# Two partial sums per PSUM bank in the wide projections of a hybrid layer, and one modulation vector accumulated on GpSimd

## The chip, the cores and the metric

The kernel runs on one core of one Trainium2 chip. The metric is the device time of one execution in microseconds, as the median of several runs. TensorE multiplies, VectorE and ScalarE work elementwise, GpSimd does small side jobs, and SyncE's queue issues nearly all loads.

## The reference

One layer of a diffusion backbone over 256 latent and 256 context tokens with 2048 channels, in float32:

```python
mod = silu_c @ w_mod[l] + b_mod[l]
sh1, sc1, g1, sh2, sc2, g2 = (t[:, None, :] for t in jnp.split(mod, 6, axis=-1))
...
hx = modulate(rms_norm(x, norm1_g[l]), sh1, sc1)
out_x, _, _ = token_mixer(hx, *mix_args, s_f, s_b, True)
x = x + g1 * out_x
x = x + g2 * conv_ffn(modulate(rms_norm(x, norm2_g[l]), sh2, sc2),
                      w_up[l], ffn_dw[l], ffn_db[l], w_down[l], True)
...
return rms_norm(x, final_g)
```

The mixer multiplies the tokens with w_in (13312 columns), runs a gated linear recurrence over eight heads in both directions (branch A) and a short convolution (branch B), projects both with w_pa and w_pb, merges them by sigmoid gates and projects with w_o. The FFN multiplies with w_up (2 x 5632 columns), convolves one half over the token grid, multiplies the halves and projects with w_down.

## The kernel before

Every weight is used once. wload asks for a raw tile of 1 MB (four buffers); wsplit cuts each half of it into an exact high part (w_hi, ScalarE, line 90) and the low rest (w_lo, VectorE, line 91), five buffers each. The tokens are kept in two such parts too: hx[:, k, 0, :] and hx[:, k, 1, :] lie side by side, 256 tokens each. A product needs three matmuls, which mm3 issues: low weights with high tokens, high weights with high tokens, high weights with low tokens. In proj the weights are stationary (128 x 128) and 256 tokens move; 16 tiles k of 128 rows sum into one PSUM tile acc of [128, 2, 256], one bank, that holds two blocks n of 128 output channels. A bank is 512 floats wide. Six banks (pool psA) rotate for all products, two (psH) serve small ones.

The program runs in stages: norm 1 and modulated gates of the first heads (zacc); four rounds g of the recurrence for two heads each (hgrn), in which gate products (acx, lines 365 to 378), q (proj, line 586) and values (vacc, moving operand 512 columns) fill TensorE between the recurrence's own small products (kdt, ps, po, pn); branch B and the branch A gate (four steps j of four proj calls); the merge (eight steps j with two branches each: one proj of 16 tiles over w_in, one of 8 over w_pa or w_pb); w_o with the residual and norm 2 (tiles to, 512 columns moving); the FFN's up projection (22 steps j, two proj calls each); w_down. A scheduler of the framework sets each engine's order within and across stages, by its own estimate of times; it is in order per engine at run time.

The second half's modulation vectors (segments 4, 3, 2, 5 of w_mod) are summed row by row: mod_steps loads a raw tile of 128 rows, VectorE adds raw times a scalar to macc (line 617), and pump advances it by one tile at places between the products. Segment 5, the gate g2, falls into the steps j = 2 to 17 of the FFN's up projection; then macc is split, spread over the partitions on TensorE and copied (lines 631 to 637).

Of the kernel before, what the change touches and what calls it, by code (L numbers as in the profile page):

```python
# [36 lines left out]
def hybrid_layer_kernel(ctx: ExitStack, tc: tile.TileContext, I, out, dbg=None):  # L37
# [9 lines left out]
    # Pools that live to the end.  # L47
# [5 lines left out]
    psA = ctx.enter_context(tc.tile_pool(name="psA", bufs=6, space=PSUM))  # L53
    psH = ctx.enter_context(tc.tile_pool(name="psH", bufs=2, space=PSUM))

# [4 lines left out]
    # ---------------------------------------------------------------- weights  # L60
# [89 lines left out]
    # =============================================================== startup  # L150
# [6 lines left out]
    # parameters as rows of 128, transposed to one value per partition  # L157
# [48 lines left out]
    # norm 1 of the latent and the context tokens, then channels on partitions  # L206
# [28 lines left out]
    # modulation of norm 1 in blocks of 256 channels, and with each block the products that it feeds:  # L235
    # backward gates of heads 0 to 3, forward gates of heads 0 to 2
# [8 lines left out]
    def mod_block(b):  # L245
        """shift and scale of block b as partial sums in 4 groups of 32 partitions"""
# [14 lines left out]
    def h_block(b, pm):  # L261
        """modulated tokens of the channels of block b"""
# [20 lines left out]
    def block_products(b, halves):  # L283
        """the products of block b, one output tile of 2 times 256 tokens at a time"""
# [40 lines left out]
    # lower bounds of the forget gates: softmax over the two rows  # L325
# [54 lines left out]
    def proj_xc1(w, c0):  # L380
        """One tile of 128 output channels for the latent and the context tokens."""
# [16 lines left out]
    def gate_evac(acc, dst):  # L398
        """sigmoid of the forget gate of one head and direction"""
        nc.scalar.activation(dst, acc[:], AF.Sigmoid)  # L400

    def q_evac(acc):
# [22 lines left out]
    def hgrn(g, ft, q):  # L425
        """Heads 2g and 2g+1. ft: sigmoids of the gates [direction, latent/context, head, token]."""
# [7 lines left out]
        # log f in two ranges of the logarithm, whose sum is exact where one is 0  # L434
# [12 lines left out]
        # final states of the context  # L447
# [29 lines left out]
        # scores [s, t] of both directions, by levels of the highest bit in which s and t differ;  # L477
        # up to the sixth level blocks of 64 by 64, two of them side by side in the array
# [25 lines left out]
        for lev in range(8):  # L504
# [28 lines left out]
            # halves join: exclusive sums take the whole of the other half, then the inclusive ones  # L533
# [31 lines left out]
    # gates of heads 2 and 3 wait in the part of v that is written last  # L565
    early = {}
    for g in range(4):
# [18 lines left out]
        q = q_evac(proj(w_in, [256 * g], hx, KD)[0])  # L586
# [22 lines left out]
    # modulations of the second half: sums over the rows within a partition, then over the partitions  # L609
    def mod_steps():  # L610
        for seg in (4, 3, 2, 5):
# [3 lines left out]
            for k in range(KD):  # L615
                raw = wload([(w_mod[k * P:k * P + P, seg * D:seg * D + D], (2048,))])
                nc.vector.scalar_tensor_tensor(out=acc[:], in0=raw[:], scalar=cst[:, k, 0:1], in1=acc[:], op0=ALU.mult, op1=ALU.add)  # L617
# [29 lines left out]
    for j in range(4):  # L647
        pc0, = proj(w_in, [6 * AW + 256 * j], hx, KD)
        u = tp.tile([P, 2, T], F32, name="u", tag="u")
        nc.scalar.copy(u[:], pc0[:])  # L650
        pump(1)
        pc1, = proj(w_in, [7 * AW + 256 * j], hx, KD)
        nc.vector.tensor_tensor(out=u[:], in0=u[:], in1=pc1[:], op=ALU.mult)
# [8 lines left out]
        nc.vector.tensor_tensor(out=cv[:], in0=cv[:], in1=pc2[:], op=ALU.mult)  # L662
        split((y_b[:, 2 * j:2 * j + 2, 0, :], y_b[:, 2 * j:2 * j + 2, 1, :]), cv[:])
        pump(1)
        pc3, = proj(w_in, [4 * AW + 256 * j], hx, KD)
        sg = tp.tile([P, 2, T], F32, name="sg", tag="sg")
        nc.scalar.activation(sg[:], pc3[:], AF.Sigmoid)
        nc.vector.tensor_tensor(out=sg[:], in0=sg[:], in1=pc3[:], op=ALU.mult)
# [6 lines left out]
    # merge of the branches  # L675
    w_pa = I["w_pa"][0]
    w_pb = I["w_pb"][0]
    for j in range(8):
        mb = []
        for i, (c0, w, y) in enumerate(((8 * AW, w_pa, y_a), (8 * AW + D, w_pb, y_b))):  # L680
            pg, = proj(w_in, [c0 + 256 * j], hx, KD)
            sg = tp.tile([P, 2, T], F32, name=f"sm{i}", tag=("u", "cv")[i])
            last_sigmoid = nc.scalar.activation(sg[:], pg[:], AF.Sigmoid)
            pump(2)
            pp, = proj(w, [256 * j], y, 8)
            nc.vector.tensor_tensor(out=sg[:], in0=sg[:], in1=pp[:], op=ALU.mult)
# [5 lines left out]
    tp_cm.__exit__(None, None, None)  # L692

    # ============================================================ w_o, the residual and norm 2
# [82 lines left out]
    def warm_sqrt(after):  # L777
        """the table of the square root, loaded while nothing waits for it"""
# [48 lines left out]
    # ============================================================ gated conv FFN  # L827
# [5 lines left out]
    for j in range(NF // 2):  # L833
# [4 lines left out]
        nc.scalar.copy(av[:], pa_[:])  # L838
# [93 lines left out]
```

## Time and profile before

| what | value |
|---|---|
| runs | 1776.76, 1777.16, 1778.48 us (median 1777.16) |
| span of the profiled execution | 1776.6 us |
| TensorE busy | 1746.4 us (98%), 13207 matmuls |
| VectorE busy | 1263.8 us (71%) |
| ScalarE busy | 857.3 us (48%) |
| GpSimd busy | 21.3 us (1%) |
| HBM | 381.20 MB read, 216 GB/s over the span |
| mean granted TensorE clock | 0.993 |

The profiled execution is known by its span alone, from its first to its last instruction; the median of the runs lies 0.6 us above it. A row of a group reads: line, engine, operation, output<-input, shapes, count, then busy time and mean length of one, then idle time of the engine ahead of it and what ended it. Matmul rows overlap each other, so a matmul's length is no pace. A row of a timeline begins with start and length in us.

### The profile page before, as it was taken

Reading aid. Unit: us, or ns where it says so; the run is one execution under the profiler, and the core shown is the slowest. Engines: PE = TensorE matmul, PEld = TensorE weight load, DVE = VectorE, ACT = ScalarE, POOL = GpSimd, SP = SyncE. Lnnn points to the kernel's source line nnn. Section 1 sums busy time; section 2 is a strip of 40 time slices with the busy share of each in tenths; the row PEclk is TensorE's granted clock in tenths of the full one; section 3 lists DMA queues with packets and bytes.
Section 4 is the critical chain, followed back from the end, with each engine's and each line's share of the span. In section 5 each row is a group of like instructions: output and inputs, shape, how many; then the busy total and the mean of one; then the engine's idle time right before and its main releaser. Section 6 shows DMA issues by size and latency. Waiting matters only on the chain.

```text
span 1776.6 us, 31077 instructions
## 1 busy us (share of the span) xinstructions
PE 1746.4 (98%) x13207; PEld 1641.1 (92%) x13207; DVE 1263.8 (71%) x1601; ACT 857.3 (48%) x1062; POOL 21.3 (1%) x26
## 2 busy tenths in 40 slices
PE   5999999999999999999999999999999999999998
PEld 3779889999999999999998899999999999888887
DVE  4337276677998768767865588778778877877774
ACT  4226255466555434434454454444444454665553
POOL 0000000000000000000000000000000000000000
PEclk9999999999999999999999999999999999999999
DMA  9996224223877879879976367767766755555552
GB/s 334 345 331 211 95 72 119 72 96 119 284 239 254 271 244 310 295 257 313 313 278 215 119 215 236 231 224 234 238 227 225 236 190 190 190 190 190 196 192 86
DMA packets 289008, 385.30 MB, mean 217 GB/s; under 512 B 7812, under 2 KB 241581, under 8 KB 280038
## 3 DMA queue, kind: packets, MB, share of 16 engines
q1 hardware_dynamic: 287872, 379.82, 64.3%
q10 hardware_dynamic: 694, 3.24, 0.5%
q8 instruction: 103, 1.69, 0.4%
q0 software_dynamic: 304, 0.26, 0.1%
q14 instruction: 35, 0.29, 0.0%
HBM read 381.20 MB, written 2.10 MB: 216 GB/s over the span
## 4 chain that ended last, share of the span: by engine, by line
PE 98%; DMA 0%; ACT 0%; DVE 0%; issue 0%; SPq 0%; ACTq 0%
PE acc L110 57%; PE to L110 19%; PE acx L110 6%; PE vacc L110 5%; PE zacc L110 5%; PE pm L110 2%; PE ps L110 2%; PE po L110 1%; PE pt L225 1%; DMA xt<-in_x_dram 0%; PE pc L110 0%; PE kdt L463 0%; PE ptx L798 0%; ACT hx L213 0%; PE pn L110 0%
## 5 line engine op out<-in xcount | busy, mean ns | idle before, releaser
L110 PE MATMUL acc<-hx,w_hi 128*128 128x256 f32 x5120 | 928.4, 284 | 0.0
L91 DVE TENSOR_TENSOR w_lo<-raw,w_hi 128x1024 fp32r<-128x1024 f32 (+1 forms) x521 | 633.4, 1219 | 269.7 <-ACT w_hi L90 266.2
L90 ACT ACTIVATE w_hi<-raw 128x1024 fp32r<-128x1024 f32 (+1 forms) x522 | 549.5, 1054 | 562.4 <-PE acc L110 360.4
L110 PEld LDWEIGHTS acc<-hx,w_hi 128*128 128x128 f32 x5120 | 802.9, 193 | 0.8
L110 PE MATMUL acc<-hx,w_lo 128*128 128x256 f32 x2560 | 727.9, 284 | 1.4 <-ACT hx L815 1.4
L110 PEld LDWEIGHTS acc<-hx,w_lo 128*128 128x128 f32 x2560 | 494.0, 193 | 1.9 <-issue 1.6
L110 PE MATMUL to<-w_hi,hx 128*128 128x512 f32 (+1 forms) x792 | 221.6, 366 | 0.0
L617 DVE SCALAR_TENSOR_TENSOR macc<-raw,cst,macc 128x2048 f32<-128x2048 f32 x64 | 150.3, 2348 | 30.6 <-DMA raw<-in_w_mod_dram 22.7
L110 PEld LDWEIGHTS to<-w_hi,hx 128*128 128x128 f32 x792 | 142.9, 188 | 24.4
L853 DVE SCALAR_TENSOR_TENSOR cvf<-av,pf,cvf 128x189 f32<-128x189 f32 (+2 forms) x352 | 132.6, 429 | 35.7 <-ACT cvf L841 35.7
L110 PE MATMUL to<-w_lo,hx 128*128 128x512 f32 (+1 forms) x396 | 145.1, 366 | 0.0
L106 ACT ACTIVATE hx<-y 128x512 fp32r<-128x512 f32 x88 | 55.5, 631 | 89.2 <-PE to L110 87.0
L110 PEld LDWEIGHTS to<-w_lo,hx 128*128 128x128 f32 x396 | 74.6, 188 | 12.0
L107 DVE TENSOR_TENSOR hx<-y,hx 128x512 fp32r<-128x512 f32 x88 | 60.7, 692 | 34.1 <-ACT hx L106 34.1
L110 PE MATMUL to<-w_hi,mg 128*128 128x512 f32 (+1 forms) x288 | 82.0, 368 | 0.0
L110 PE MATMUL acx<-hx,w_hi 128*128 128x256 f32 x288 | 61.1, 289 | 0.0
L110 PEld LDWEIGHTS to<-w_hi,mg 128*128 128x128 f32 x288 | 51.8, 188 | 8.7
L110 PE MATMUL acx<-hc,w_hi 128*128 128x256 f32 x288 | 58.6, 285 | 0.0
L110 PE MATMUL to<-w_lo,mg 128*128 128x512 f32 (+1 forms) x144 | 52.8, 366 | 0.0
L110 PE MATMUL zacc<-hx,w_hi 128*128 128x256 f32 x224 | 52.2, 289 | 0.0
L110 PE MATMUL acc<-y_b,w_hi 128*128 128x256 f32 x256 | 47.9, 289 | 0.0
L110 PE MATMUL zacc<-hc,w_hi 128*128 128x256 f32 x224 | 47.1, 287 | 0.0
(229 smaller groups left out, 1771.7 us busy)
## 6 DMA issues: line engine op xcount, KB each, us to landing
raw<-in_w_up_dram SPq DMA_DIRECT2D x88, 1024.0 KB, 5.2
raw<-in_w_in_dram SPq DMA_DIRECT2D x81, 1024.0 KB, 5.9
raw<-in_w_mod_dram SPq DMA_DIRECT2D x64, 1024.0 KB, 6.4
raw<-in_w_down_dram SPq DMA_DIRECT2D x44, 1024.0 KB, 5.0
raw<-in_w_mod_dram SPq DMA_DIRECT2D x64, 512.0 KB, 6.9
raw<-in_w_o_dram SPq DMA_DIRECT2D x16, 1024.0 KB, 5.4
raw<-in_w_in_dram SPq DMA_DIRECT2D x24, 512.0 KB, 4.3
raw<-in_w_pa_dram SPq DMA_DIRECT2D x8, 1024.0 KB, 5.8
```

The source lines that it names most:

```text
L90: nc.scalar.activation(hi[:, :n], half, AF.Copy)
L91: sub.tensor_tensor(out=lo[:, :n], in0=half, in1=hi[:, :n].bitcast(F32), op=ALU.subtract)
L106: nc.scalar.activation(dst[0], src, AF.Copy)
L107: nc.vector.tensor_tensor(out=dst[1], in0=src, in1=dst[0].bitcast(F32), op=ALU.subtract)
L110: return nc.tensor.matmul(o, lhsT, rhs, start=start, stop=stop, skip_group_check=True)
L225: nc.tensor.transpose(pt[:, k, :], xts[2 * i + t][k4 // 2][:, kk * P:kk * P + P], ident[:])
L617: nc.vector.scalar_tensor_tensor(out=acc[:], in0=raw[:], scalar=cst[:, k, 0:1], in1=acc[:], op0=ALU.mult, op1=ALU.add)
L853: nc.vector.scalar_tensor_tensor(out=c4[:, ro, co], in0=a4[:, ri, ci], scalar=pf[:, tap * NF + f:tap * NF + f + 1], in1=c4[:, ro, co], op0 ...
```

## The change

mm2 takes the place of mm3 in proj: one matmul of the high weights over both token parts (512 columns, a whole bank), and one of the low weights over the high tokens (256 columns), which adds to the second half of that bank. A product therefore leaves two sums side by side, and an accumulator of two blocks n takes two banks. joined brings the sums together: ScalarE copies the second, VectorE adds the first. The gate products and values keep mm3 and psA's six banks; q has a projection of its own, proj_q, with one bank per block; from the end of the recurrence on, the six banks are three double ones (psW), again six single ones for w_o (psB), three double ones for the FFN's up projection (psF) and six for w_down (psD). The convolution's first tap in branch B moves to ScalarE. For segment 5, GpSimd scales the raw tile in place and adds it to macc.

```diff
+    def mm2(o, wl, wh, s, start, stop):
+        mm(o, wh, s, start, False)
+        mm(o[:, T:2 * T], wl, s[:, 0, :], False, stop)
+
+    def joined(dst, acc):
+        nc.scalar.copy(dst, acc[:, :, 1, :])
+        nc.vector.tensor_tensor(out=dst, in0=acc[:, :, 0, :], in1=dst, op=ALU.add)
...
     def proj(w, cols, src, kt):
-            acc = psA.tile([P, 2, T], F32, name="acc", tag="acc")
+            acc = psW.tile([P, 2, 2, T], F32, name="acc", tag="acw")
...
                         for n in range(2):
-                            mm3(acc[:, n, :], lv[:, n * P:n * P + P], hv[:, n * P:n * P + P],
-                                src[:, kk, 1, :], src[:, kk, 0, :], kk == 0 and n == 0, kk == kt - 1)
+                            mm2(acc[:, n].rearrange("p a b -> p (a b)"), lv[:, n * P:n * P + P], hv[:, n * P:n * P + P],
+                                src[:, kk], kk == 0, kk == kt - 1)
+    def proj_q(c0):
+        accs = []
+        for n in range(2):
+            acc = psA.tile([P, 2, T], F32, name="acc", tag="acc")
+            accs.append(acc)
...
+    def q_evac(accs):
         q = gp.tile([P, 2, T], F32, name="q", tag="q", bufs=2)
-        nc.scalar.activation(q[:], acc[:], AF.Sigmoid)
-        nc.vector.tensor_tensor(out=q[:], in0=q[:], in1=acc[:], op=ALU.mult)
+        for n, acc in enumerate(accs):
+            nc.scalar.copy(q[:, n, :], acc[:, 1, :])
+            nc.vector.tensor_tensor(out=q[:, n, :], in0=acc[:, 0, :], in1=q[:, n, :], op=ALU.add)
+        sg = g2.tile([P, 2, T], F32, name="sq", tag="qq")
+        nc.scalar.activation(sg[:], q[:], AF.Sigmoid)
+        nc.vector.tensor_tensor(out=q[:], in0=q[:], in1=sg[:], op=ALU.mult)
...
+    psA_cm.__exit__(None, None, None)
+    psW_cm, psW = banks("psW", 3)
...
-                nc.vector.scalar_tensor_tensor(out=acc[:], in0=raw[:], scalar=cst[:, k, 0:1], in1=acc[:], op0=ALU.mult, op1=ALU.add)
+                if seg == 5:
+                    nc.gpsimd.tensor_scalar(out=raw[:], in0=raw[:], scalar1=cst[:, k, 0:1], scalar2=None, op0=ALU.mult)
+                    nc.gpsimd.tensor_tensor(out=acc[:], in0=raw[:], in1=acc[:], op=ALU.add)
+                else:
+                    nc.vector.scalar_tensor_tensor(out=acc[:], in0=raw[:], scalar=cst[:, k, 0:1], in1=acc[:], op0=ALU.mult, op1=ALU.add)
...
-            nc.vector.tensor_scalar(out=cv[:, n, :], in0=u[:, n, :], scalar1=w[1], scalar2=None, op0=ALU.mult)
+            nc.scalar.activation(cv[:, n, :], u[:, n, :], AF.Copy, scale=w[1])
...
-        nc.scalar.copy(av[:], pa_[:])
+        joined(av[:], pa_)
...
-        nc.vector.tensor_tensor(out=yj, in0=yj, in1=pb_[:], op=ALU.mult)
+        bv = tw.tile([P, 2, T], F32, name="bv", tag="bv")
+        joined(bv[:], pb_)
+        nc.vector.tensor_tensor(out=yj, in0=yj, in1=bv[:], op=ALU.mult)
```

Every other product of proj is joined in the same way (into u, z or sg) before its first use.

The order of VectorE in round g = 3 of the recurrence, from the last gate (ft, line 431, line 465 after) to the operand of the transposes kdt (line 457, line 491 after). Its middle, before:

```order
L563 TENSOR_TENSOR o_n<-po,r 128x512
L91 TENSOR_TENSOR w_lo<-raw,w_hi 128x1024
L405 TENSOR_TENSOR q<-q,acc 128x512
L91 TENSOR_TENSOR w_lo<-raw,w_hi 128x1024
L443 TENSOR_TENSOR X<-X,ft 128x1024
L444 TENSOR_TENSOR gc<-gc,ft 128x1024
L91 TENSOR_TENSOR w_lo<-raw,w_hi 128x1024 x2
L617 SCALAR_TENSOR_TENSOR macc<-raw,cst,macc 128x2048
L449 MEMSET ft 128x2
L537 TENSOR_TENSOR X<-X 128x2x256
L91 TENSOR_TENSOR w_lo<-raw,w_hi 128x1024
```

The same piece after:

```order
L597 TENSOR_TENSOR o_n<-po,r 128x512
L96 TENSOR_TENSOR w_lo<-raw,w_hi 128x1024
L436 TENSOR_TENSOR q<-acc,q 128x256
L96 TENSOR_TENSOR w_lo<-raw,w_hi 128x1024
L436 TENSOR_TENSOR q<-acc,q 128x256
L477 TENSOR_TENSOR X<-X,ft 128x1024
L478 TENSOR_TENSOR gc<-gc,ft 128x1024
L657 SCALAR_TENSOR_TENSOR macc<-raw,cst,macc 128x2048
L439 TENSOR_TENSOR q<-q,sq 128x512
L483 MEMSET ft 128x2
L571 TENSOR_TENSOR X<-X 128x2x256
```

From the row kt (line 433, line 467 after) to the operand of kdt there were 11 rows of w_lo and 3 of macc; now there are 6 and 2, and q's sum takes two adds more. On TensorE, 344 matmuls of proj stood between the end of the gate products acx and kdt (line 463); now 68 pairs do.

The order of TensorE at the end of the FFN's up projection, where the first tiles of the down projection (to00, to10) begin, with the engines waited for. Before:

```order
L110 MATMUL acc_15814<-hx_97,w_lo_15904 128x256
L110 MATMUL acc_15814<-hx_97,w_hi_15903 128x256 x2
L110 MATMUL to00_15941<-w_hi_15945,hx_97 128x512 [waits Activation_49]
L110 MATMUL to00_15941<-w_lo_15946,hx_97 128x512 [waits DVE_49]
L110 MATMUL to00_15941<-w_hi_15945,hx_97 128x512 [waits DVE_49]
L110 MATMUL to10_15942<-w_hi_15945,hx_97 128x512 [waits PE_49]
```

After:

```order
L115 MATMUL acc_13287<-hx_97,w_hi_13352 128x512
L115 MATMUL acc_13287<-hx_97,w_lo_13353 128x256
L115 MATMUL to00_13389<-w_hi_13393,hx_97 128x512 [waits DVE_49,Activation_49]
L115 MATMUL to00_13389<-w_lo_13394,hx_97 128x512
L115 MATMUL to00_13389<-w_hi_13393,hx_97 128x512 [waits DVE_49]
L115 MATMUL to10_13390<-w_hi_13393,hx_97 128x512 [waits DVE_49]
```

A trio has become a pair of 512 and 256 columns, and the first matmul of to10 now waits for VectorE: its bank belonged to acc_13287, the last product of the stage, and is free when that is joined.

The order of VectorE in one step j of the FFN's up projection. Before:

```order
L853 SCALAR_TENSOR_TENSOR cvf<-av,pf,cvf 128x3x63 x2
L617 SCALAR_TENSOR_TENSOR macc<-raw,cst,macc 128x2048
L91 TENSOR_TENSOR w_lo<-raw,w_hi 128x1024
L859 TENSOR_TENSOR y<-y,cvf 128x512
L91 TENSOR_TENSOR w_lo<-raw,w_hi 128x1024
L860 TENSOR_TENSOR y<-y,acc 128x512
L91 TENSOR_TENSOR w_lo<-raw,w_hi 128x1024 x2
L853 SCALAR_TENSOR_TENSOR cvf<-av,pf,cvf 128x4x63 x4
```

After:

```order
L132 TENSOR_TENSOR bv<-acc,bv 128x512
L906 SCALAR_TENSOR_TENSOR cvf<-av,pf,cvf 128x3x63
L96 TENSOR_TENSOR w_lo<-raw,w_hi 128x1024
L912 TENSOR_TENSOR y<-y,cvf 128x512
L915 TENSOR_TENSOR y<-y,bv 128x512
L96 TENSOR_TENSOR w_lo<-raw,w_hi 128x1024 x3
L132 TENSOR_TENSOR av<-acc,av 128x512
L96 TENSOR_TENSOR w_lo<-raw,w_hi 128x1024
L906 SCALAR_TENSOR_TENSOR cvf<-av,pf,cvf 128x4x63 x4
```

The macc row is gone and two joins (line 132) have come in; GpSimd's queue has 16 times one row of line 654 and one of line 655 in its place.

More of the change, by code (lines that the diff above doesn't have):

```diff
@@ L52, in hybrid_layer_kernel, with banks @@
     hxp = ctx.enter_context(tc.tile_pool(name="hxp", bufs=1))
-    psA = ctx.enter_context(tc.tile_pool(name="psA", bufs=6, space=PSUM))
     psH = ctx.enter_context(tc.tile_pool(name="psH", bufs=2, space=PSUM))
+    def banks(name, n):
+        cm = tc.tile_pool(name=name, bufs=n, space=PSUM, reuse_waits="tile")
+        return cm, cm.__enter__()
+    psA_cm, psA = banks("psA", 6)
     def dump(name, ap):
@@ L585, in hybrid_layer_kernel @@
                     gate_evac(acc, ft[:, 1 - d, :, n, :])
-        q = q_evac(proj(w_in, [256 * g], hx, KD)[0])
+        q = q_evac(proj_q(256 * g))
         if g == 0:
@@ L649, in hybrid_layer_kernel @@
         u = tp.tile([P, 2, T], F32, name="u", tag="u")
-        nc.scalar.copy(u[:], pc0[:])
+        joined(u[:], pc0)
         pump(1)
         pc1, = proj(w_in, [7 * AW + 256 * j], hx, KD)
-        nc.vector.tensor_tensor(out=u[:], in0=u[:], in1=pc1[:], op=ALU.mult)
+        z = tp.tile([P, 2, T], F32, name="z", tag="z")
+        joined(z[:], pc1)
+        nc.vector.tensor_tensor(out=u[:], in0=u[:], in1=z[:], op=ALU.mult)
         cv = tp.tile([P, 2, T], F32, name="cv", tag="cv")
@@ L661, in hybrid_layer_kernel @@
         pc2, = proj(w_in, [5 * AW + 256 * j], hx, KD)
-        nc.vector.tensor_tensor(out=cv[:], in0=cv[:], in1=pc2[:], op=ALU.mult)
+        z = tp.tile([P, 2, T], F32, name="z", tag="z")
+        joined(z[:], pc2)
+        nc.vector.tensor_tensor(out=cv[:], in0=cv[:], in1=z[:], op=ALU.mult)
         split((y_b[:, 2 * j:2 * j + 2, 0, :], y_b[:, 2 * j:2 * j + 2, 1, :]), cv[:])
@@ L665, in hybrid_layer_kernel @@
         pc3, = proj(w_in, [4 * AW + 256 * j], hx, KD)
+        z = tp.tile([P, 2, T], F32, name="z", tag="z")
+        joined(z[:], pc3)
         sg = tp.tile([P, 2, T], F32, name="sg", tag="sg")
-        nc.scalar.activation(sg[:], pc3[:], AF.Sigmoid)
-        nc.vector.tensor_tensor(out=sg[:], in0=sg[:], in1=pc3[:], op=ALU.mult)
+        nc.scalar.activation(sg[:], z[:], AF.Sigmoid)
+        nc.vector.tensor_tensor(out=sg[:], in0=sg[:], in1=z[:], op=ALU.mult)
         nc.vector.scalar_tensor_tensor(out=sg[:], in0=o_n[:, 2 * j:2 * j + 2, :], scalar=ang, in1=sg[:], op0=ALU.mult, op1=ALU.mult)
@@ L682, in hybrid_layer_kernel @@
             sg = tp.tile([P, 2, T], F32, name=f"sm{i}", tag=("u", "cv")[i])
-            last_sigmoid = nc.scalar.activation(sg[:], pg[:], AF.Sigmoid)
+            joined(sg[:], pg)
+            last_sigmoid = nc.scalar.activation(sg[:], sg[:], AF.Sigmoid)
             pump(2)
             pp, = proj(w, [256 * j], y, 8)
-            nc.vector.tensor_tensor(out=sg[:], in0=sg[:], in1=pp[:], op=ALU.mult)
+            z = tp.tile([P, 2, T], F32, name="z", tag="z")
+            joined(z[:], pp)
+            nc.vector.tensor_tensor(out=sg[:], in0=sg[:], in1=z[:], op=ALU.mult)
             mb.append(sg)
@@ L692, in hybrid_layer_kernel @@
     tp_cm.__exit__(None, None, None)
+    psW_cm.__exit__(None, None, None)
+    psA_cm, psA = banks("psB", 6)
     xp = ctx.enter_context(tc.tile_pool(name="xp", bufs=1, side="right", reuse_waits="tile"))
@@ L825, in hybrid_layer_kernel @@
     onp.__exit__(None, None, None)
+    psA_cm.__exit__(None, None, None)
+    psW_cm, psW = banks("psF", 3)
     yfp = ctx.enter_context(tc.tile_pool(name="yfp", bufs=1, reuse_waits="tile"))
@@ L865, in hybrid_layer_kernel @@
     pump(1)
+    psW_cm.__exit__(None, None, None)
+    psA_cm, psA = banks("psD", 6)
     td = ctx.enter_context(tc.tile_pool(name="td", bufs=2, reuse_waits="tile"))
```

11 lines of the change are left out of this document (9 added, 2 removed).

## The prediction

> **What bounds the kernel now.** I read the busy shares and the chain of work on the page first, then the pieces of that chain in order of time, then groups by shape, and last the timelines of the places where the change could meet a wait.
>
> ```profile
> PE 1746.4 (98%) x13207; PEld 1641.1 (92%) x13207; DVE 1263.8 (71%) x1601; ACT 857.3 (48%) x1062; POOL 21.3 (1%) x26
> PE 98%; DMA 0%; ACT 0%; DVE 0%; issue 0%; SPq 0%; ACTq 0%
> ```
>
> The chain is TensorE from end to end, so a microsecond taken from TensorE's stream counts unless another engine becomes late. A busy TensorE is not TensorE at its peak, so I take its pace from pieces of the chain: time over matmuls.
>
> ```profile
> 168.04 43.55 PE vacc L110 x192
> 280.40 11.51 PE acc L110 x96
> 1016.98 439.49 PE acc L110 x3648
> ```
>
> Matmuls of 256 columns pass every 11.51/96 = 119.9 ns, in the long FFN stretch every 120.5 ns; those of 512 columns every 43.55/192 = 226.8 ns. The line through both has 0.418 ns a column and a fixed 13.0 ns for each instruction. So three matmuls of 256 columns (359.7 ns) carry as many columns as one of 512 and one of 256 (346.7 ns), with one fixed cost more.
>
> **The change part by part.** *Matmuls.* Every call of mm3 inside proj becomes a pair. Each trio has one matmul with the low weights, so these rows count the trios:
>
> ```profile
> L110 PE MATMUL acc<-hx,w_lo 128*128 128x256 f32 x2560 | 727.9, 284 | 1.4 <-ACT hx L815 1.4
> L110 PE MATMUL acc<-y_b,w_lo 128*128 128x256 f32 x128 | 37.0, 289 | 0.0
> L110 PE MATMUL acc<-y_a,w_lo 128*128 128x256 f32 x128 | 36.3, 283 | 0.0
> ```
>
> 2560 + 128 + 128 = 2816 trios at 13.0 ns are 36.6 us. All lie in TensorE's stream, so I book the whole gain and take off what the change makes late. Had the 120.5 ns stood for the trio, it would be 41 us; some of that is clock (below), so I keep 36.6. The Trainium skill ("TensorE: Matmul & The Clock Gate", section "Back-to-back issue gap") gives a fixed 2.5 ns for a warm matmul; by it the gain would be an estimated 2816 x 2.5 ns = 7 us. The rows here, with a weight load before every matmul, show 13.0 ns, and they decide.
>
> *Last gate block of the recurrence.* The scheduler now puts less filler before the transposes kdt of the fourth head pair. Before:
>
> ```profile
> 415.90 6.22 PE acx L110 x52
> 422.36 1.42 PE acc L110 x12
> 424.01 39.82 PE acc L110 x332
> 463.67 1.04 PE L463 MATMUL kdt<-ident,ft 128*128 128x128 f32 x8
> 422.16 0.60 ACT L400 ACTIVATE ft<-acx 128x512 f32<-128x512 f32 x1 [1.22 <-PE acx L110]
> 424.31 1.23 DVE L433 TENSOR_SCALAR kt<-ft 128x2048 f32<-128x2048 f32 x1
> 434.99 2.35 DVE L91 TENSOR_TENSOR w_lo<-raw,w_hi 128x1024 fp32r<-128x1024 f32 x2
> 445.26 2.35 DVE L617 SCALAR_TENSOR_TENSOR macc<-raw,cst,macc 128x2048 f32<-128x2048 f32 x1
> 458.47 1.23 DVE L457 TENSOR_TENSOR ft<-ft,kt 128x1024 f32<-128x1024 f32 x1
> ```
>
> The last gate product ends at 422.1, kdt starts 41.5 us later, and what kdt needs (L457) is written at 459.7, 37.6 us later: 3.9 us to spare. VectorE is back to back from 424.31 to 459.7, 35.4 us, with 11 w_lo and 3 macc in it (the order shows this). Afterwards there are 6 w_lo and 2 macc, and q's sum is two adds: 35.4 - 5 x 1.14 (a pair of w_lo takes 2.35 with the one behind it starting 2.27 later) - 2.3 + 0.7 = 28.1 us, ready 30.3 us after the last gate product. TensorE has 68 pairs (23.6 us) and two pn (0.4 us) there: 24.0 us. It would wait 6 us. After a hole the clock falls too:
>
> ```profile
> 631.88 3.96 PE pc L110 x32
> 632.00:660.00 28.00, 28.00 (x211) 28.00 (x212) 19.93 (x16) 10.01 (x11) 2.32 (x2) 0.88 0.69 232
> ```
>
> Four microseconds of one-column matmuls were followed by a mean granted clock of 0.88 over 28 us, 3.4 us lost, so I add 1 us for the hole. Loss taken 7 us; ends 0 (the scheduler's filler suffices) and 10 us.
>
> *FFN edges.* At the FFN's start the first matmul now streams both parts of hx, so it waits for VectorE's L818 behind ScalarE's L815; at the end the second tile of the down projection gets the bank of the very last up product, whose release now takes w_hi (ahead of it on ScalarE), the copy and VectorE's add.
>
> ```profile
> L815 ACT ACTIVATE hx<-xg,sh 128x256 fp32r<-128x256 f32 x16 | 7.2, 498 | 1.7 <-DVE xg L813 1.7
> L818 DVE SCALAR_TENSOR_TENSOR hx<-xg,sh,hx 128x256 fp32r<-128x256 f32 x16 | 7.0, 481 | 0.0
> L838 ACT COPY av<-acc 128x512 f32<-128x512 f32 x22 | 12.9, 585 | 40.2 <-PE acc L110 40.2
> L860 DVE TENSOR_TENSOR y<-y,acc 128x512 f32<-128x512 f32 x22 | 15.0, 682 | 0.4
> L90 ACT ACTIVATE w_hi<-raw 128x1024 fp32r<-128x1024 f32 x514 | 542.9, 1057 | 562.2 <-PE acc L110 360.4 <-DMA raw<-in_w_in_dram 40.0 <-PE to L110 39.1
> ```
>
> Start: 0.6 us. End: 1.06 + 0.59 + 0.68 + 0.1 of handover, less three matmuls of 0.227 already possible: 1.8 us. Other releases have two products of time (three accumulators rotate), so I cost them at nothing: cover gone only if VectorE falls 11 us behind.
>
> *Merge.* One branch of one step has 48 trios and loads five raw tiles of 1 MB; as pairs it shrinks from 48 x 0.3597 = 17.3 us to 16.6 us.
>
> ```profile
> 830.00:860.00 30.00, 30.00 (x253) 30.00 (x252) 24.01 (x20) 11.85 (x13) 0.00 (x0) 1.00 0.91 311
> raw<-in_w_mod_dram SPq DMA_DIRECT2D x27, 1024.0 KB, 8.3
> ```
>
> The DMA engines are 0.91 busy at 311 GB/s; 4% more asks for 0.95. The four raw buffers turn in 4 x 3.3 us against 8.3 us to landing, so it should fit: 1 us, ends 0 and 10 (the merge's whole gain). ScalarE and VectorE take the joins (0.6 us each a product) inside their idle time there.
>
> *FFN up with GpSimd.* VectorE loses the macc step and gains two joins a step of j; GpSimd gets a scaling and an add.
>
> ```profile
> 1100.48 1.72 DVE L853 SCALAR_TENSOR_TENSOR cvf<-av,pf,cvf 128x252 f32<-128x252 f32 x4 [1.59 <-ACT cvf L841]
> 1110.92 2.35 DVE L617 SCALAR_TENSOR_TENSOR macc<-raw,cst,macc 128x2048 f32<-128x2048 f32 x1
> 1117.82 1.23 DVE L91 TENSOR_TENSOR w_lo<-raw,w_hi 128x1024 fp32r<-128x1024 f32 x1 [1.05 <-ACT w_hi L90]
> 1120.71 1.23 DVE L91 TENSOR_TENSOR w_lo<-raw,w_hi 128x1024 fp32r<-128x1024 f32 x1 [1.67 <-ACT w_hi L90]
> 1123.52 0.93 DVE L853 SCALAR_TENSOR_TENSOR cvf<-av,pf,cvf 128x252 f32<-128x252 f32 x2 [1.58 <-ACT cvf L841]
> L91 POOL TENSOR_TENSOR w_lo<-raw,w_hi 128x1024 fp32r<-128x1024 f32 x1 | 2.4, 2397 | 86.1 <-ACT w_hi L90 86.1
> L578 POOL COPY ft<-v 128x512 f32<-128x512 f32 x3 | 1.7, 611 | 8.2 <-PE po L110 8.2
> ACT w_hi L90 <- PE acc L110: 364.4, 232, 6.6
> ```
>
> A step lasts 23.04 us with 4.3 idle, so VectorE works 18.7; afterwards 18.7 - 2.3 + 1.3 = 17.7 of TensorE's 64 pairs = 22.2 us: 4.5 to spare. Freeing VectorE is therefore worth nothing by itself. GpSimd takes about 2 x 2.4 + 4 x 0.57 = 7.1 us a step, far under 22.2; a step has five loads, one each 4.4 us, so one of the four raw buffers is wanted again after 18 us, and GpSimd gives it back some 12 us after the load is issued (5 us to land, 7 of work); SP's queue, which would stand behind that buffer, stays clear. ScalarE splits the finished sum 14 split halves (39 us) after the last load can be issued, so that does not wait either. The one open question is whether GpSimd's reads slow VectorE: in the trace VectorE is idle in both GpSimd rows, so nothing shows it. Ends: 0, and every GpSimd microsecond lost to VectorE: (7.1 - 4.5) x 16 steps = 42 us, less the lead of four split halves (4 x 2.8 us; ScalarE waiting for TensorE's releases shows that splits run ahead) = 31 us. I take 1, near the free end, since the spare 4.5 us and the lead absorb up to 5.2 us a step.
>
> Sum on the profiled span 1776.6: 36.6 - 7 - 0.6 - 1.8 - 1 - 1 = 25.2 us, giving 1751.4; the runs' median 1777.16 lies 0.6 us above the span, so 1752.
>
> **The rivals.** *Contention.* GpSimd and VectorE exclude each other for 5.2 to 6.9 us a step: 0 to 28 us lost, 1751 to 1779, its middle 1765. Against it: nothing in these rows. For it: nearly all of VectorE's work in that stage (splits, taps, products) reads two SBUF operands. The Trainium skill ("SBUF — State Buffer", section "Who interferes with whom") says just that a VectorE instruction with two SBUF inputs and a GpSimd instruction that reads SBUF lock each other out for a whole instruction; no run here shows it yet.
>
> *Slower.* The same place, but GpSimd's instructions stretch while they fight for the port: from (25.2 + 1 + 11)/16 + 4.5 = 6.8 us of exclusion a step the gain is gone; at 9 us it is (9 - 4.5) x 16 - 11 = 61 us against 26, about 1812.
>
> *Clean.* kdt and merge wait for nothing: 36.6 - 2.4 gives 1743.
>
> *Nothing gained.* If the fixed 13 ns belonged to the weight switch of a kind that a 512 column matmul followed by one of 256 still pays thrice, the matmuls would save nothing and the waits of 11.4 us remain: about 1788. Against it: 512 column matmuls in the trace already switch weights each time.
>
> **How the numbers follow.** Forecast case (matmul gain less the waits, contention absorbed, 1746 to 1757) 0.52; clean (1740 to 1746) 0.14; contention 0.25; slower 0.05; nothing gained 0.02; merge bound by DMA (about 1761) 0.02. The range takes the forecast case, most of the clean one and contention up to 18 us: 1742 to 1770. About 0.2% (3.6 us) is what a measurement of this kernel tells from no change: faster 0.89, same 0.04 (the top of contention), slower 0.07.
>
> **What would show it.** The acc rows fall to 2816 matmuls of 512 and 2816 of 256 columns, a 64 pair product takes 11.1 us, and the FFN stretch 488 us. A hole of about 6 us stands before the fourth kdt; one of about 2 us before the first down tile. GpSimd's two rows measure 2.3 and 4.8 us; contention would show as w_lo and cvf rows longer than 1.23 us and 0.43 us (four in 1.72) during them and as TensorE waiting for w_lo from about the tenth step of j on. The prediction fails if 512 column matmuls in pairs run off 226.8 ns, or if VectorE is late.

## The result, and the profile after

The changed kernel takes 1794.8 us (the middle of three runs, 1794.66 to 1795.49) against 1777.6 before: slower, ratio 1.0098, interval 1.0083 to 1.0113. A fourth execution took 6021.9 us, is counted as slow and left out of every comparison. The forecast was 1752 and faster. The profiled execution has a span of 1792.9 us.

The busy line of the page after, and the chain of work that ended last by engine:

```profile
PE 1730.4 (97%) x10391; PEld 1491.4 (83%) x10391; DVE 1389.9 (78%) x1677; ACT 886.4 (49%) x1142; POOL 188.0 (10%) x58
PE 80%; DVE 14%; issue 5%; ACT 0%; DMA 0%; SPq 0%; DVEq 0%; ACTq 0%
```

TensorE issues 2816 matmuls fewer and is busy only 16 us less. VectorE is busy 126 us more, although it lost 16 macc steps (38 us), and 14% of the chain now runs over it, with 5% in which it waits for nothing that the profile shows. The list of waits after (engine, line, what it waited for, us in total, times, longest) names the places:

```profile
PE acc L115 <- DVE w_lo L96: 20.6, 15, 1.8
PE acc L115 <- DVE q L436: 7.0, 1, 7.0
...
PE to L115 <- DVE bv L132: 3.7, 1, 3.7
...
PE acc L115 <- DVE hx L869: 2.7, 2, 1.8
```

Before, none of these four was there; at the FFN's start TensorE waited 1.4 us, for ScalarE's hx. The first is the FFN's up projection, the second the recurrence, the third and fourth the two ends of the FFN stage.

**The FFN stage.** The timeline of VectorE and of GpSimd in one step after:

```profile
1233.19 0.40 DVE L906 SCALAR_TENSOR_TENSOR cvf<-av,pf,cvf 128x189 f32<-128x189 f32 x1
1233.52 0.68 DVE L132 TENSOR_TENSOR bv<-acc,bv 128x512 f32<-128x512 f32 x1
1234.12 3.19 DVE L906 SCALAR_TENSOR_TENSOR cvf<-av,pf,cvf 128x189 f32<-128x189 f32 x1
1237.23 1.21 DVE L96 TENSOR_TENSOR w_lo<-raw,w_hi 128x1024 fp32r<-128x1024 f32 x1
1238.37 0.68 DVE L912 TENSOR_TENSOR y<-y,cvf 128x512 f32<-128x512 f32 x1
1239.08 5.01 DVE L915 TENSOR_TENSOR y<-y,bv 128x512 f32<-128x512 f32 x1
...
1232.98 5.85 POOL L654 TENSOR_SCALAR raw<-raw,cst 128x2048 f32<-128x2048 f32 x1 [13.65 <-DVE cvf L906]
1238.92 4.63 POOL L655 TENSOR_TENSOR macc<-raw,macc 128x2048 f32<-128x2048 f32 x1
...
1263.13 4.64 POOL L655 TENSOR_TENSOR macc<-raw,macc 128x2048 f32<-128x2048 f32 x1
```

The product y of line 915, 0.69 us when nothing disturbs it, starts 0.16 us after GpSimd's addition and ends 0.5 us after it: 4.3 us of its 5.01 it stood still. A tap of 0.40 us took 3.19 during GpSimd's scaling. Each step has these two places, 7.1 us together. The join of line 132, which reads PSUM and one SBUF operand, ran in its usual 0.68 us inside the scaling; so did a tap, a w_lo and a y near the ends of the scaling, so the scaling blocks for about half of its 5.85 us (2.8 us on the tap) and the addition for all of its 4.63. The table of windows for 100 us of this stage, before and then after (busy us and instructions of PE, PEld, DVE, ACT, POOL, then PE clock, DMA share, GB/s):

```profile
1200.00:1300.00 100.00, 100.00 (x836) 100.00 (x835) 82.20 (x119) 45.31 (x52) 0.00 (x0) 1.00 0.71 231
```

```profile
1200.00:1300.00 100.00, 94.95 (x532) 82.15 (x531) 99.86 (x119) 44.81 (x56) 41.73 (x8) 0.98 0.66 222
```

VectorE went from 82 to 99.9 of 100 us and TensorE began to wait. A step lasts 24.2 us (from one addition of GpSimd to the next), where the pairs alone need 22.2 to 22.6.

**The pairs.** The chain of work from 780 to 880 us (the merge), one piece in each kernel; first before, then after, with a later piece of after from the end of the FFN's up projection:

```profile
779.99 100.08 PE acc L110 x834
```

```profile
779.99 100.23 PE acc L115 x567
...
1474.94 53.37 PE acc L115 x302
```

Before, 834 matmuls are 278 trios of 360.0 ns. After, 567 are 283.5 pairs of 353.5 ns, and 302 are 151 of 353.4: 6.6 ns saved a trio where 13.0 were forecast. But between 640 and 760 us, and in most of the disturbed steps of the FFN, the starts of successive pairs stand 346.7 ns apart. The pace has two values, keeps one for hundreds of matmuls, and in these traces changes only at breaks of the stream.

**The recurrence.** The 7.0 us are not where the prediction put them. The timeline after of TensorE (its row with the idle time ahead of it) and of VectorE, and then the piece of the chain behind the wait:

```profile
439.88 0.79 PE L115 MATMUL acc<-hx,w_hi 128*128 128x512 f32 x1 [7.03 <-DVE q L436]
...
437.94 0.42 DVE L436 TENSOR_TENSOR q<-acc,q 128x256 f32<-128x256 f32 x1
438.28 1.21 DVE L96 TENSOR_TENSOR w_lo<-raw,w_hi 128x1024 fp32r<-128x1024 f32 x1
439.41 0.42 DVE L436 TENSOR_TENSOR q<-acc,q 128x256 f32<-128x256 f32 x1
```

```profile
439.88 15.07 PE acc L115 x71
```

The first product of the second phase got the double bank one half of which held q of the fourth head pair, and waited until VectorE, late, had read it. The transposes kdt then found their operand ready. Of the 15.07 us behind the wait, 71 matmuls at 353.4 ns a pair are 12.5; 2.5 us went to a slower clock: the granted clock reads 0.50 from 438.2 to 444.7 us, still in the wait at first, and 1.00 from 444.9 on.

### The profile page after: what moved, and what is told of

Same layout as the page of the kernel before. It is cut to its first block, busy times and chain, and to the rows that moved or that the text cites. A ratio compares the mean times of both kernels' runs of the same rounds, so it can differ in the third digit from the quotient of the medians.

```text
span 1792.9 us, 25774 instructions
## 1 busy us (share of the span) xinstructions
PE 1730.4 (97%) x10391; PEld 1491.4 (83%) x10391; DVE 1389.9 (78%) x1677; ACT 886.4 (49%) x1142; POOL 188.0 (10%) x58
## 4 chain that ended last, share of the span: by engine, by line
PE 80%; DVE 14%; issue 5%; ACT 0%; DMA 0%; SPq 0%; DVEq 0%; ACTq 0%
PE acc L115 40%; PE to L115 19%; DVE w_lo L96 6%; PE acx L115 6%; DVE cvf L906 5%; PE vacc L115 5%; PE zacc L115 5%; PE pm L115 2%; PE ps L115 2%; PE po L115 1%; PE pt L241 1%; DMA xt<-in_x_dram 0%; DVE bv L132 0%; DVE y L912 0%; PE pc L115 0%
## 5 line engine op out<-in xcount | busy, mean ns | idle before, releaser
L115 PE MATMUL acc<-hx,w_hi 128*128 128x512 f32 x2560 | 908.7, 399 | 9.7 <-DVE q L436 7.0
L115 PE MATMUL acc<-hx,w_lo 128*128 128x256 f32 x2560 | 723.7, 283 | 20.6 <-DVE w_lo L96 20.6
L115 PEld LDWEIGHTS acc<-hx,w_hi 128*128 128x128 f32 x2560 | 484.1, 189 | 124.7 <-DVE q L436 7.4
L115 PEld LDWEIGHTS acc<-hx,w_lo 128*128 128x128 f32 x2560 | 487.5, 190 | 26.3 <-DVE w_lo L96 25.7
L906 DVE SCALAR_TENSOR_TENSOR cvf<-av,pf,cvf 128x189 f32<-128x189 f32 (+2 forms) x352 | 179.8, 565 | 0.0
L657 DVE SCALAR_TENSOR_TENSOR macc<-raw,cst,macc 128x2048 f32<-128x2048 f32 x48 | 112.6, 2346 | 27.9 <-DMA raw<-in_w_mod_dram 22.7
L654 POOL TENSOR_SCALAR raw<-raw,cst 128x2048 f32<-128x2048 f32 x16 | 92.1, 5757 | 269.3 <-DMA raw<-in_w_mod_dram 141.2
L915 DVE TENSOR_TENSOR y<-y,bv 128x512 f32<-128x512 f32 x22 | 80.1, 3641 | 0.7
L655 POOL TENSOR_TENSOR macc<-raw,macc 128x2048 f32<-128x2048 f32 x16 | 74.5, 4654 | 1.3
L911 ACT ACTIVATE y<-cvf 128x512 f32<-128x512 f32 x22 | 13.9, 631 | 116.1 <-DVE cvf L906 116.1
L894 ACT ACTIVATE cvf<-av,pf 128x256 f32<-128x256 f32 x44 | 24.0, 593 | 86.2 <-DVE av L132 86.2
```

Source lines behind the costliest of these rows:

```text
L115: return nc.tensor.matmul(o, lhsT, rhs, start=start, stop=stop, skip_group_check=True)
L654: nc.gpsimd.tensor_scalar(out=raw[:], in0=raw[:], scalar1=cst[:, k, 0:1], scalar2=None, op0=ALU.mult)
L655: nc.gpsimd.tensor_tensor(out=acc[:], in0=raw[:], in1=acc[:], op=ALU.add)
L894: nc.scalar.activation(cv[:, n, :], av[:, n, :], AF.Identity, scale=pf[:, 4 * NF + f:4 * NF + f + 1], bias=pf[:, 9 * NF + f:9 * NF + f + 1])
L906: nc.vector.scalar_tensor_tensor(out=c4[:, ro, co], in0=a4[:, ri, ci], scalar=pf[:, tap * NF + f:tap * NF + f + 1], in1=c4[:, ro, co], op0 ...
L915: nc.vector.tensor_tensor(out=yj, in0=yj, in1=bv[:], op=ALU.mult)
```

## The experiments

Three theories stood. *Lock*: GpSimd's reads shut VectorE out, and VectorE has no room for it. *Pairs*: the pair itself, with its joins, is what cost the time. *Edges*: single waits on banks. The price in the changed kernel was to be split among them.

### GpSimd's part undone

```
-                if seg == 5:
-                    nc.gpsimd.tensor_scalar(...); nc.gpsimd.tensor_tensor(...)
-                else:
+                nc.vector.scalar_tensor_tensor(out=acc[:], in0=raw[:], scalar=cst[:, k, 0:1], in1=acc[:], ...)
```

> The changed kernel with the last modulation vector accumulated on VectorE again, the wide matmuls kept. Theory (GpSimd and VectorE exclude each other in the FFN): VectorE works 17.7 + 2.35 = 20.0 us of a step that TensorE needs 22.2 to 22.7 us for, so TensorE's 15 waits for w_lo (20.6 us) and the slow clock behind them (about 3 us) go: 1769 to 1774. What stays is the wait before the transposes of the fourth head pair (7 us and 3 us of slow clock) and the FFN's two edges. Rival (the wide matmuls or the joins are what makes the FFN stage slow): 1790 or more.

Measured 1768.6 us (1764.7 to 1771.3), ratio to before 0.9950 (0.9933 to 0.9968). That is just under the 1769 to 1774 of the theory, and the rival's 1790 is out. The GpSimd part costs 26 us, 24 to 30 by the spread of these runs. The same window, and the chain over the merge:

```profile
1200.00:1300.00 100.00, 100.00 (x568) 86.67 (x567) 85.74 (x126) 48.88 (x58) 0.00 (x0) 1.00 0.72 236
```

```profile
779.87 100.18 PE acc L115 x578
```

VectorE does more instructions in less time, and TensorE never waits. Here the merge ran at 200.36/578 = 346.6 ns a pair: the same code as in the changed kernel, the other pace. That may be why the runs of this kernel lie 6.6 us apart; each kernel has one trace, so it is not shown.

### GpSimd's part alone, on the kernel before

```
+                if seg == 5:
+                    nc.gpsimd.tensor_scalar(...); nc.gpsimd.tensor_tensor(...)
```

> The kernel before with only the GpSimd part: its matmuls as they were, the last modulation vector on GpSimd. Theory (exclusion of about 7 us a step): VectorE has 18.7 - 2.35 + 7.0 = 23.4 us of work or locked time in a step of 23.04, 0.3 us too much in each of 16 steps, which the lead of the splits covers: 1777 to 1783, with taps or products of several us beside GpSimd's instructions in the rows. Rival (GpSimd slows TensorE or the transfers themselves): 1795 or more. Rival (no exclusion, the wide matmuls made VectorE late): 1777 and no long row on VectorE.

Measured 1778.7 us, ratio 1.0008 (0.9999 to 1.0018): no change that can be told, as the theory had it. Its window, and a row of its VectorE timeline where three w_lo stand beside GpSimd's two instructions:

```profile
1200.00:1300.00 100.00, 100.00 (x835) 100.00 (x835) 99.58 (x118) 43.12 (x52) 42.28 (x8) 1.00 0.69 233
```

```profile
1208.34 10.66 DVE L91 TENSOR_TENSOR w_lo<-raw,w_hi 128x1024 fp32r<-128x1024 f32 x3
```

Three w_lo take 3.5 us undisturbed; 7.2 us are lock. VectorE is at 99.6% as in the changed kernel, and yet TensorE, which needs 23.04 us a step here, waits for w_lo just once, for 0.3 us. Most of the additions stand 23.1 and 23.5 us apart in turn, 0.3 us a step more than TensorE needs, which the lead of the splits pays: 16 steps were just few enough. The lock is the same in both kernels; what the wide matmuls add is that VectorE has two joins more and TensorE 0.4 to 0.8 us less a step.

### GpSimd's addition done twice

```
                     nc.gpsimd.tensor_tensor(out=acc[:], in0=raw[:], in1=acc[:], op=ALU.add)
+                    nc.gpsimd.tensor_tensor(out=raw[:], in0=raw[:], in1=acc[:], op=ALU.add)
```

> The kernel before with the last modulation vector on GpSimd and a second addition of GpSimd behind the first in each step (into a buffer that is then given back, so no value changes). Theory (each microsecond of GpSimd's addition is one that VectorE is locked out): the lock grows from 7.2 to some 11.7 us a step, VectorE has 16.35 + 11.7 = 28.0 us against TensorE's 23.04, 16 steps of 5.0 less a lead of 11: about 69 us, 1830 to 1860. Rival (GpSimd and VectorE share the port by turns and the first 7 us were a start-up price): below 1800.

Measured 1854.7 us, ratio 1.0436 (1.0419 to 1.0454). Against the run with one addition, 76 us more; the added instruction takes 16 x 4.91 = 78.6 us.

```profile
L620 POOL TENSOR_TENSOR raw<-raw,macc 128x2048 f32<-128x2048 f32 x16 | 78.6, 4912 | 1.3
```

Of the 76 us, TensorE's waits for w_lo are 48.3; the granted clock fell too, from 0.995 to 0.979. VectorE sets the step: most scalings there start 28.0 to 28.3 us apart, some 5 us more than with one addition. Once VectorE is full, a microsecond of GpSimd's addition is nearly a microsecond of the kernel. By the SBUF page of the Trainium skill ("SBUF — State Buffer", section "Who interferes with whom") a VectorE instruction with two SBUF inputs and a GpSimd instruction that reads SBUF shut each other out for the whole instruction. The runs agree for the addition; for the scaling, which has one SBUF input, the rows above show about half.

### GpSimd's scaling alone

```
                     nc.gpsimd.tensor_scalar(out=raw[:], in0=raw[:], scalar1=cst[:, k, 0:1], ...)
-                    nc.gpsimd.tensor_tensor(out=acc[:], in0=raw[:], in1=acc[:], op=ALU.add)
```

> The changed kernel with GpSimd only scaling the rows of the last modulation vector; the addition, and so the sum, is left out. Theory (GpSimd holds the port for about 2.7 us of the scaling): VectorE has 17.7 + 2.7 = 20.4 us in a step of 22.2 to 22.7, TensorE does not wait, 1766 to 1773, as with VectorE accumulating. Rival (any GpSimd instruction in this stage delays the w_lo that stands next): waits of w_lo stay and the time is above 1778.

Measured 1770.0 us (1763.3 to 1772.8), within the spread the time of the kernel with no GpSimd part. The window:

```profile
1200.00:1300.00 100.00, 100.00 (x579) 88.15 (x578) 92.18 (x127) 49.80 (x60) 25.11 (x4) 1.00 0.74 247
```

GpSimd works 25 us of the 100 at no price that can be told, and no wait for w_lo is left: VectorE still has 8 us. With the runs above this fits a price that begins where VectorE's idle time ends.

### Scaling on ScalarE, addition on GpSimd

```
-                    nc.gpsimd.tensor_scalar(out=raw[:], in0=raw[:], scalar1=cst[:, k, 0:1], ...)
+                    nc.scalar.activation(raw[:], raw[:], AF.Copy, scale=cst[:, k, 0:1])
```

> The changed kernel with the scaling of the last modulation vector on ScalarE and only the addition on GpSimd. Theory (VectorE is locked out for the whole time that GpSimd works, 4.4 us of the addition): VectorE has 17.7 + 4.4 = 22.1 us in a step of 22.2 to 22.7, so TensorE waits little, and the time is that of the kernel with no GpSimd part within 4 us. Rival (the price is per GpSimd instruction or a stall that any GpSimd work sets off): half of the 21 us of waits stay, 1780 to 1786. Rival (ScalarE, with 2 us more a step, makes the splits late): waits for w_hi on VectorE and TensorE, 1780 or more.

Measured 1785.6 us, ratio 1.0046 (1.0029 to 1.0063): the theory missed, in the range of both rivals, 17 us over the kernel without GpSimd. Of TensorE's 20.6 us of waits for w_lo 14.3 stayed. Rows of ScalarE and VectorE in one step:

```profile
1203.13 2.01 ACT L654 ACTIVATE raw<-raw,cst 128x2048 f32<-128x2048 f32 x1 [5.35 <-DMA raw<-in_w_mod_dram]
...
1206.11 4.87 DVE L96 TENSOR_TENSOR w_lo<-raw,w_hi 128x1024 fp32r<-128x1024 f32 x1 [2.80 <-ACT w_hi L95]
```

ScalarE stood 5.35 us behind the load of the row block, w_hi came late, VectorE idled 2.8 us, and then ran into the lock with the next w_lo (3.7 us). Two things were changed at once, so the run does not tell what the addition alone would cost; it shows that an in-order engine that is given a load to wait for passes the wait on.

### Two wide, two narrow

```
-                        for n in range(2):
-                            mm2(acc[:, n]..., lv[...], hv[...], src[:, kk], kk == 0, kk == kt - 1)
+                        for n in range(2):
+                            mm(av_[n], hv[...], src[:, kk], kk == 0, False)
+                        for n in range(2):
+                            mm(av_[n][:, T:2 * T], lv[...], src[:, kk, 0, :], False, kk == kt - 1)
```

> As the kernel with VectorE accumulating, and the two output tiles of a row tile interleaved: two matmuls of 512 columns, then two of 256, instead of 512, 256, 512, 256. In the changed kernel a pair passes every 353.3 ns in some stretches and every 346.7 ns in others. Theory (the extra 6.7 ns is paid where a 512 column matmul is followed by one of 256 and back, each time): half as many changes, 350 ns or 346.7, 5 to 15 us faster than the kernel with VectorE accumulating. Rival (the extra belongs to something outside the order of the matmuls): same within 3 us. Rival (a load of weights is too long to hide behind 256 columns when two come in a row): slower, 120 ns becoming more.

Measured 1760.2 us (1759.8 to 1760.9), ratio 0.9905 (0.9890 to 0.9920): 8.5 us less than with 512 and 256 columns in turn, and the runs lie 1.1 us apart instead of 6.6.

```profile
779.78 100.32 PE acc L115 x576
```

200.64/576 = 348.3 ns a pair, and the starts of the pairs show 348.3 in every stretch of the proj products. So the order of the widths matters and the slow pace of 353.4 is gone. The theory's mechanism is not confirmed: a fixed price for each change of width would give 350 or 346.7, and the same order of 512 and 256 in turn also ran at 346.7. What puts a run of pairs into one pace or the other was not found.

### The first bank of the second phase

```
     psW_cm, psW = banks("psW", 3)
+    skip = psW.tile([P, 2, 2, T], F32, name="skip", tag="acw")
+    nc.vector.memset(skip[:, 0, 0, 0:1], 0.0)
```

> As the kernel with two wide and two narrow matmuls in turn, and the rotation of the double banks of the second phase shifted by one (a one column memset takes the first), so that its first product takes a bank that the fourth head pair's q has not used. The wait of 7.0 us that the trace of the changed kernel shows for q's sum is a matmul of the product pc0 waiting for that bank. Theory (a second wait stands behind the first: TensorE comes to the fourth kdt 24 us after the last gate product, VectorE writes kdt's operand 30.3 us after it): the wait moves to kdt and is about 6 us there, 1757 to 1761. Rival (the bank was all): the 7 us and 3 us of slow clock behind it go, 1750.

Measured 1763.5 us (1763.3 to 1768.5), 3.3 more than without, which is outside the range given by 2.5; the kernel before was 1.1 us slower in this measurement too.

```profile
452.28 1.97 PE L499 MATMUL kdt<-ident,ft 128*128 128x128 f32 x8 [6.16 <-DVE ft L493]
```

With the bank free, TensorE comes to kdt and waits there 6.2 us: the wait of the prediction, at its place and of its size. In the changed kernel the wait on q stands ahead of it and hides it. The shift of the banks also gave w_o's first matmul a wait of 1.9 us.

### All waits at once

On top of the last two: q's products as two wide and two narrow; the fourth kdt queued behind two products of the second phase (96 pairs instead of 68); the down projection's first tiles in banks of the second last up product; three narrow matmuls for the first 8 row tiles of the FFN's first product.

```
+            for ins in moved:                      # the transposes of the fourth head pair
+                tc.add_manual_dep(ins.ins, tail[0].ins.name, ...)
+    for _ in range(3):                             # ahead of the down projection
+        skip = psA.tile([P, 512], F32, name="skip", tag="acc"); nc.vector.memset(skip[:, 0:1], 0.0)
```

> All of it together, without the GpSimd part: two wide and two narrow matmuls in turn, also for q; the double banks shifted by one; the transposes of the fourth head pair queued behind two products of the second phase (96 pairs, 33 us, instead of 68); the down projection's first two tiles in banks that the second last up product has left; in the FFN's first product the first 8 row tiles with three matmuls of 256. Theory: of the 1760 of the kernel with two wide and two narrow in turn go 7.0 + 3 (wait and clock in the recurrence), 3.7 + 3 (down projection), 1 to 2 (FFN start) and 1 (q): 1741 to 1745. Rival (VectorE is still later: more splits stand ahead of kdt's operand): a wait of 3 to 6 us at kdt, 1746 to 1750.

Measured 1756.7 us (1753.5 to 1759.1), 3.4 less than with two wide and two narrow alone, where 15 to 19 were expected; the rival's 1746 to 1750 was missed too. The waits of TensorE:

```profile
PE ps L115 <- DVE ke L562: 4.2, 1, 4.2
...
PE acc L115 <- DVE w_lo L96: 3.2, 1, 3.2
...
PE to L115 <- DVE z L132: 1.9, 1, 1.9
```

The FFN's end has no wait left and its start 1.9 us, against 1.4 before the change. In the recurrence the wait was only moved again: VectorE has too much work between the last gate product and the scores, and stands behind loads of macc besides.

### VectorE relieved in the first quarter

```
-        pump(1)
+        pump((0, 2, 2, 2)[j])     # and (0, 1, 1, 2), (0, 1, 1, 1), (0, 1, 1, 1) at the other three places
```

and three skipped banks ahead of w_o's tiles, as above.

> As the kernel with all of it together, and two more: the first quarter of the second phase has no step of the modulation vectors (its four steps go to the other three quarters), so VectorE has neither macc's 2.3 us each nor its waits for the loads there; and w_o's first tiles take banks that the last merge product has left. Theory (what was left are VectorE's macc steps and their waits): the waits of 3.2 and 4.2 us in the recurrence and of 1.9 us before w_o go, with about 1 us of slow clock: 1744 to 1750. Rival (the loads moved to the other quarters make VectorE late there): 1753 or more.

Measured 1759.6 us (1759.3 to 1761.5), where 1744 to 1750 were expected: not faster than before this edit, and in the rival's range for another reason than the rival's. The waits in the recurrence and before w_o are gone, and the FFN's first product waits:

```profile
PE acc L115 <- DVE xg L883: 14.4, 1, 14.4
```

The skipped banks had moved rb, which VectorE reads until its last xg, into the bank of the FFN's first product. The same kernel without these skipped banks:

> As e13_order, but w_o's tiles take the banks that they had before that edit. There the FFN's first product took the bank of rb, which VectorE reads until its last product of xg, and TensorE waited 14.4 us with 8.6 us of slow clock behind it; here rb has another bank. Theory (that collision was the whole difference): 1759.6 less 14.4 and 8.6, plus 1.9 for the wait of w_o and 1 to 2 of clock: 1739 to 1745. Rival (the wait on xg has another cause, the narrow matmuls of the FFN's first product): 1755 or more.

Measured 1749.7 us (1748.8 to 1751.0), ratio to before 0.9844 (0.9830 to 0.9857). The collision was the cause; the repair gave 9.8 us, not the 15 to 21 expected. The long piece of the chain in the FFN, with the collision and without:

```profile
1013.38 426.68 PE acc L115 x2464
```

```profile
1004.37 426.82 PE acc L115 x2464
```

The two are equally long, so the wait had cost no more clock than stands there without it. The low mean clock read from the window around the long wait (0.57 from 1000 to 1020 us) counted the wait itself: the granted clock is 0.50 from 1002.1 to 1019.0 us, but the product starts at 1013.4; without the collision it is 0.50 from 1004.4 to 1010.2 us, and the product starts at 1004.4. So 5.6 and 5.8 us of matmuls run at half clock. This kernel beats both the kernel before and the changed one; its chain is TensorE to 97%.

### GpSimd's part on the reordered kernel

The kernel of the section above with rb's collision, and segment 5 on GpSimd as in the change; the wait of 14.4 us stands in both.

> The kernel just before in this call with the last modulation vector on GpSimd as in the change: the second part of the change alone, where no other wait is left. Theory (exclusion): a step of the FFN goes from 22.3 us to 24.2, 16 steps of 1.9 less a lead of some 10 us and with 3 us of slow clock: 20 to 27 us slower than without. Rival (the price in the change came from its other waits too): less than 10 us.

Measured 1794.6 us against 1759.6 without: 35 us, more than either theory gave.

```profile
PE acc L115 <- DVE w_lo L96: 24.2, 12, 3.6
```

24.2 us are waits for w_lo. The mean granted clock of the profiled executions fell from 0.991 to 0.984, which over 1790 us is another 12.5; the two profiled spans, 1794.2 and 1758.0 us, differ by 36.2. By the pieces of the chain 34.2 of that lie in the FFN stage, 529.7 us (from 1015.29 to 1544.98) against 495.4 (from 1013.38 to 1508.83). The price of the lock does not come from the change's other waits; with pairs of 348.3 ns in the FFN it is larger than in the change, where the trace without GpSimd's part has most pairs of that stage at 353.4.

## Why the prediction was wrong

The forecast span was 1751.4, the measured one 1792.9: 41.5 us. By steps, with what was booked and what the runs show:

| step | booked us | shown us | from |
|---|---|---|---|
| matmuls | -36.6 | -24 | an estimate from the pairs of the interleaved kernel, 2816 x (360.0 - 348.3) = 33, less its 8.5 over pairs in turn |
| GpSimd in the FFN | +1 | +26 | change against the run with that part undone |
| wait in the recurrence | +7 | +9.5 | 7.0 and 2.5 of clock |
| FFN start | +0.6 | +1.3 | waits for hx L869, 2.7, less the 1.4 before |
| FFN end | +1.8 | +6 | 3.7, and 243.8 instead of 241.4 us for the down products behind it |
| merge, DMA | +1 | 0 | its pairs pass at the pace of other stages |

The differences add up to 44, 2.5 more than the gap; the pace of the pairs differs from trace to trace of the same code, and the runs of the kernel with that part undone lie 6.6 us apart. The traces of these two kernels differ by 23.6 us: 20.7 lie between the FFN's first long piece and w_down (525.7 us against 505.0), and 2.7 ahead of it, where GpSimd's part does not run and the pace of the merge differs.

*GpSimd* is the step that turned the sign. The rival "slower" was named, with its mechanism, and given 0.05. The upper end of the term (every GpSimd microsecond lost, 31 us) was near the truth, with 7.1 us locked a step. That both have the figure 7.1 is luck: the forecast meant the whole of GpSimd's work, which came to 10.4 us, of which VectorE lost 7.1. The failure is the sentence "I take 1, near the free end, since the spare 4.5 us and the lead absorb up to 5.2 us a step". It decided by what the kernel could absorb, not by what the rows said the lock could be; no row stood near the free end. VectorE's own work was nearly right (24.2 - 7.1 = 17.1 us a step against 17.7), and the runs fit a threshold where the arithmetic had it: with wide matmuls, 25 us of GpSimd in 100 cost nothing that can be told, 42 do. The GpSimd instructions themselves took 5.76 and 4.65 us, not 2.3 and 4.8. Why the scaling takes so long is not shown; where it was GpSimd's only work it took 5.7 to 7.7 us too.

*The matmuls*: the fixed cost of 13.0 ns was right for one pace (346.7) and twice too large for the other (353.4). The line through 256 columns in a row and 512 in a row could not show what a change of width costs; a row with both, in turn, was not in the trace. (The "64 pair product" of 11.1 us is one of 64 matmuls, 32 pairs, and the 41 us for a trio at 120.5 ns each come to 41.7.) The rival "nothing gained" stood for a loss of this kind but only at its full size. By the 2.5 ns that the Trainium skill ("TensorE: Matmul & The Clock Gate", section "Back-to-back issue gap") gives for an isolated matmul, the gain was an estimated 7 us; the runs disagree: 11.7 ns a trio in groups, and 27.4 us for the whole kernel, without GpSimd's part, once most of its waits were gone.

*The recurrence*: a wait of the size booked, in another place. The prediction looked for what kdt needs and costed the release of q's bank at nothing; both are the same lateness of VectorE, and the earlier one shows. *FFN end*: the release of the bank was seen, but ScalarE's and VectorE's queue ahead of it was counted short: splits of hx, taps and w_lo stand before that join. TensorE waited 3.7 us for it, and the down products behind it took longer, before and after:

```profile
1527.43 241.40 PE to L110 x1188
```

```profile
1541.28 243.82 PE to L115 x1185
```

## What to carry to other kernels

An engine with 4.5 us to spare per step has room for 4.5 us of locks, not for "some" contention: when work moves to GpSimd beside VectorE instructions with two SBUF operands, book all of its additions as VectorE time, and about half of a scaling with one SBUF input, and check that against the step. When one wait is taken away, look for the next one on the same late engine before booking the gain: here q's bank, kdt and the scores showed 7.0, 6.2 and 4.2 us in turn, until VectorE had less to do. Matmuls of two widths are worth issuing in groups of one width: here that gave 8.5 us.

## What the runs showed of the hardware

Matmuls of 512 and 256 columns in turn pass at 346.7 or at 353.4 ns a pair, for hundreds of pairs at a time; in groups of two of each the pace was 348.3. After a wait of 7.0 us the next 15 us of TensorE took 2.5 us longer than their matmuls, with a granted clock of 0.50 up to 444.7 us, 4.8 us behind the wait's end; after the wait of 14.4 us no loss could be told from that of the kernel without it. VectorE's instructions with two SBUF operands stood still for 4.3 us of GpSimd's addition of 4.63 us and for 2.8 us of its scaling of 5.85 us; its join, with one operand in PSUM, ran in its usual 0.68 us inside the scaling.
